# A hybrid decoder layer on one core: the first feed-forward takes seven products from group 2 and one down projection behind its groups, with its side work spread over the groups and the tables on GpSimd

## The chip, the cores and the metric

One core of a Trainium2 chip runs the whole layer in one launch. The metric is the device time in microseconds (us). The engines are TensorE (PE, with its weight loads apart as PEld), VectorE (DVE), ScalarE (ACT), GpSimd (POOL) and SyncE (SP), which issues nearly all transfers.

## The reference

Width 1024, 1024 tokens, feed-forward width 2816, one batch, float32 in and out.

```python
def swiglu(h, w_gate, w_up, w_down):
    return (jax.nn.silu(h @ w_gate) * (h @ w_up)) @ w_down
...
    c_act = jax.nn.silu(cond)
    mod = c_act @ w_mod[l] + b_mod[l]
    (sh1, sc1, g1, sh2, sc2, g2, sh3, sc3, g3) = jnp.split(mod, N_MOD, axis=-1)

    h = modulate(rms_norm(x, ffn1_norm[l]), sh1, sc1)
    x = x + 0.5 * g1[:, None, :] * swiglu(h, ffn1_w_gate[l], ffn1_w_up[l], ffn1_w_down[l])

    h = modulate(rms_norm(x, mix_norm[l]), sh2, sc2)
    proj = h @ w_in[l]
    b_gate, c_gate, v, u = jnp.split(proj, [D_CONV, 2 * D_CONV, 3 * D_CONV], axis=-1)
    y_conv = short_conv_mixer(b_gate, c_gate, v, conv_w[l])
    y_ssm = s5_mixer(u, lambda_re[l], lambda_im[l], log_dt[l], b_re, b_im, c_re, c_im, d_skip, glu_w, glu_b)
    y_mix = jnp.concatenate([rms_norm(y_conv, out_norm_conv[l]), rms_norm(y_ssm, out_norm_ssm[l])], axis=-1)
    x = x + g2[:, None, :] * (y_mix @ w_out[l])

    h = modulate(rms_norm(x, ffn2_norm[l]), sh3, sc3)
    x = x + 0.5 * g3[:, None, :] * swiglu(h, ffn2_w_gate[l], ffn2_w_up[l], ffn2_w_down[l])
    return rms_norm(x, final_norm)
```

`s5_mixer` is a diagonal state-space model over 32 groups of 16 channels with 64 states each; its discretized matrices follow from the inputs `lambda_re`, `lambda_im`, `log_dt`, `b` and `c`, so the kernel computes tables of them before the mixer. `mod` needs `w_mod`, 36 MB.

## The kernel before, in words

**Layout.** Activations lie with the model width on the partitions: `x[k][h]` is the k-th of 8 blocks of 128 rows by 512 tokens, `h` the half of the tokens; two blocks share a tile `xt[k // 2][h]`.

**A product.** Every value is split in a high part that the multiplier keeps exactly and a low rest. `mm3` makes a product of three matmuls, high by high, high by low, low by high, into one PSUM bank, and then ticks a clock. The split costs ScalarE a cast (`hi`) and VectorE a subtraction (`lo`). `Weights` does this as a stream: `load` brings raw weights on SP's queue into two buffers, `pump` splits them into the slots of a ring (`ringp`, three granules of 128x1024, for one stretch a fourth in `ring1`) as soon as `free` returns a slot.

**Groups.** A feed-forward runs over 11 groups of two column blocks of 128. A *direct* group makes gate and up with 192 matmuls of 128x512 (`gate_up`). A group in *seven products* (`seven`) multiplies 2x2 blocks by Strassen's scheme: seven products with sums of the activation's blocks (S1 to S4, made once by `combos`), and sums of weights, which `combine` makes on GpSimd with three operations per raw tile (one of 128x1024, two of 128x512); 168 matmuls per group, with the results added together on VectorE. After each group comes its part of the down projection: 96 matmuls (`down`, `down2`), added to `x`.

**The two feed-forwards differ.** `SEVEN_FROM = (6, 1)`: the first (FFN1) is direct in groups 0 to 5 and in seven products from 6; the second (FFN2) is direct in group 0 alone. FFN2 also has its down projection behind all groups (`down7`): the products' left blocks and their sums are stored to DRAM per group (`Left`), the sums of `w_down` are made on GpSimd per group (`right_sums`) and stored, and then seven passes (`PASSES`) of 11 blocks by four banks by three matmuls, 924, read both back.

**Side work.** `Clock` orders it: a generator in `clock.side` advances one step every `clock.period` products, and `clock.after(n, fn)` calls a function n products later. FFN1's `side1` has a period of 2 during groups 1 to 3: `ssm_base` makes the basic vectors of the state-space tables, then eight times `ssm_batch` (a batch of four state groups: `bb`, `cl`, `bl`, their products `kp` and transposes `tp` on TensorE, then the rotations `rot`) and three `mod_block`, each of two modulation vectors of 128x1024. All of this arithmetic is on VectorE. The gate G1 comes in the prologue (`gate1`).

```python
    clock.period = 2
    first_seven = SEVEN_FROM[0]
    for g in range(1, first_seven):
        ...
            clock.side.append(combos(act1, "h1", "BBBA", nc.gpsimd))
```

Each engine runs its instructions in the order written here, so the engine queues follow the code. Names in the profile: `fa` is FFN1 and `fb` FFN2 with the group's number behind, `g`, `u`, `d` gate, up and down, `A`, `B`, `C` the banks of the seven products, `D` the down projection behind the groups; `w` a split weight, `raw` a raw one, `sums` its sums, `wd` a piece of `w_down` in `right_sums`, `wm` a block of `w_mod`. Helpers hold most instructions of VectorE, ScalarE and TensorE on one line (L107), so the names tell them apart.

Of the kernel before, what the change touches and what calls it, by code (L numbers as in the profile page):

```python
# [34 lines left out]
SEVEN_FROM = (6, 1)  # L35
# [59 lines left out]


class InOrder:


    strict = False  # L100

    def __init__(self, tc, engine):
        self.tc, self.engine, self.last = tc, engine, None

    def __getattr__(self, name):
        def call(*args, **kw):
            r = getattr(self.engine, name)(*args, **kw)  # L107
            if self.last is not None and InOrder.strict:
                info = mybir.DependencyInfo(mybir.DependencyClass.NoSync, mybir.DependencyReason.DATA)
                self.tc.add_manual_dep(r.ins, self.last.ins.name, info, reason="order of issue")  # L110
            self.last = r
            return r

        return call
# [115 lines left out]
def hymba_layer(ctx: ExitStack, tc, x_d, wm1_d, wmod_d, gu1_d, gs1_d, wd1_d, win_d, wout_d, glu_d, gu2_d, gs2_d, wd2_d, cols_d, cond_d, lam_d, bc_d, out_d):  # L230
    nc = tc.nc
    V, A, T, SP = (InOrder(tc, e) for e in (nc.vector, nc.scalar, nc.tensor, nc.sync))
# [55 lines left out]
    def stream(gu, gs, wd, m):  # L288

        joined = m == 1  # L290
        plain([a for g in range(m) for a in (gu[2 * g], gu[2 * g + 1], wd[g])][: 3 * m - joined])
        for g in range(m, NGRP):
            j = len(srcs)
            inner = m - joined < g < NGRP - 1
            srcs.extend([gs[g - m, 0], wd[g - 1], gs[g - m, 1]] if inner else [gs[g - m, 0], gs[g - m, 1]])
            seven = [(i, c) for i in (j, j + 1 + inner) for c in Weights.SEVEN]
            seven = [seven[i : i + 2] for i in range(0, 14, 2)]
            if inner:
                granules.extend(seven[:1] + [[(j + 1, 2 * q), (j + 1, 2 * q + 1)] for q in range(2)] + seven[1:])
            else:  # L300
                granules.extend(seven)
        j = len(srcs)
        srcs.extend([wd[NGRP - 2], wd[NGRP - 1]])
        granules.extend([(i, 2 * q), (i, 2 * q + 1)] for q in range(2) for i in (j, j + 1))

    stream(gu1_d, gs1_d, wd1_d, SEVEN_FROM[0])
# [145 lines left out]
    def norm_into(act, h, ss, n, name, where="A"):  # L452


        def use(bc):
            got = []
            for k in range(KT):
                clock.after(k, lambda k=k: got.append(modulated(k, h, bc, n, name, where)))
            act[h] = got
# [1204 lines left out]
```

## Time and profile before

| what | value |
|---|---|
| median of three runs | 1779.12 us (1778.97 to 2155.73) |
| profiled execution, own time | 1781.04 us |
| its span | 1779.3 us |
| PE busy | 1703.8 us, 96% |
| DVE busy | 1214.9 us, 68% |
| ACT busy | 520.4 us, 29% |
| POOL busy | 302.9 us, 17% |
| DMA | 245.52 MB, mean 138 GB/s |

The stages by time from the start of the span: prologue and the start of group 0 to 73; FFN1 to 784 (groups 0 to 3 to 351, 4 and 5 to 484, seven products from there); the mixer to about 1106; FFN2 after that, its down projection from 1548. A row of a window gives busy time and the number of instructions per engine in that stretch; a row of the waits gives who waits (engine, tile), for whom, the sum in us, how often, and the longest or the mean; a row of the groups gives shapes, count, busy time, the mean in ns, and the idle time ahead. Idle time of an engine that is not the bound costs nothing.

### The profile page before, as it was taken

To read this page: it belongs to the slowest core of one execution; us is meant where nothing else is said; L and a number is where in the kernel's file an instruction comes from. 1 tells how busy PE (TensorE), PEld (TensorE's weight loads), DVE (VectorE), ACT (ScalarE), POOL (GpSimd) and SP (SyncE) were. 2 spreads that over 40 slices of the span, in tenths; PEclk is the share of its full clock that TensorE was granted. 3 is DMA by queue.
4 is the path that set the end of the run, shared out by engine and by line. 5 is a ranking of instruction groups with operands and counts; after the bars stand their busy time and mean duration, and the time that the engine had idled before them with its cause. 6 is when DMAs were issued, how large, how long until landed. Compare 5 with 4: busy or idle time off the path is not lost.

```text
span 1779.3 us, 20370 instructions
## 1 busy us (share of the span) xinstructions
PE 1703.8 (96%) x7724; PEld 1407.8 (79%) x7724; DVE 1214.9 (68%) x2109; ACT 520.4 (29%) x765; POOL 302.9 (17%) x187
## 2 busy tenths in 40 slices
PE   4998989999999999999999999979999999999997
PEld 3786767788788888877888888858888888888887
DVE  7999999937755666573665845986676566656564
ACT  4311212112232223333122623422233232344440
POOL 0000000001512122020000021133555443201020
PEclk9998999999999999999999999989999999999998
DMA  7625565410021111313564131134454444677632
GB/s 313 230 72 178 197 218 193 167 62 30 24 71 48 48 48 58 127 48 106 180 211 124 48 118 52 63 119 162 175 186 181 152 144 165 215 267 255 245 125 95
DMA packets 102771, 245.52 MB, mean 138 GB/s; under 512 B 16913, under 2 KB 32529, under 8 KB 89362
## 3 DMA queue, kind: packets, MB, share of 16 engines
q1 hardware_dynamic: 102674, 244.23, 39.4%
q8 instruction: 60, 0.98, 0.2%
q14 instruction: 37, 0.30, 0.1%
HBM read 185.21 MB, written 54.79 MB: 135 GB/s over the span
## 4 chain that ended last, share of the span: by engine, by line
PE 74%; DVE 3%; POOL 1%; DMA 1%; ACT 1%; issue 1%; SPq 0%; DVEq 0%; ACTq 0%; POOLq 0%
PE fbDX L107 7%; PE fbDY L107 5%; PE wo L107 5%; PE b L107 2%; PE v L107 2%; PE c L107 2%; PE fa10d L107 2%; PE u L107 1%; PE fb0u L107 1%; PE fa5u L107 1%; PE fb0g L107 1%; PE fa8d L107 1%; PE fa7d L107 1%; PE fa6d L107 1%; PE fa4d L107 1%; PE fa4u L107 1%
## 5 line engine op out<-in xcount | busy, mean ns | idle before, releaser
L107 DVE TENSOR_TENSOR w<-raw,w 128x1024 fp32r<-128x1024 f32 (+1 forms) x220 | 256.6, 1179 | 123.2 <-ACT w L107 122.1
L107 ACT CAST w<-raw 128x1024 fp32r<-128x1024 f32 (+1 forms) x220 | 188.7, 873 | 513.5 <-POOL raw L170 58.1
L169 POOL TENSOR_TENSOR sums<-raw 128x1024 f32<-128x1024 f32 x30 | 80.7, 2689 | 846.8 <-PE fa5u L107 436.7
L107 PE MATMUL fbDX<-fbLh,w 128*128 128x512 f32 (+1 forms) x440 | 115.4, 349 | 0.0
L107 DVE TENSOR_TENSOR w<-sums,w 128x512 fp32r<-128x512 f32 x90 | 64.0, 729 | 44.7 <-ACT w L107 44.4
L107 PEld LDWEIGHTS fbDX<-fbLh,w 128*128 128x128 f32 x440 | 78.0, 191 | 10.4
L107 PE MATMUL fbDY<-fbLh,w 128*128 128x512 f32 x264 | 81.8, 389 | 0.0
L107 ACT CAST w<-sums 128x512 fp32r<-128x512 f32 x90 | 52.8, 619 | 95.6 <-PE fa8d L107 9.7
L107 PE MATMUL fbDX<-fbLl,w 128*128 128x512 f32 (+1 forms) x220 | 76.7, 349 | 0.0
L107 DVE TENSOR_TENSOR fbLl<-fbLr,fbLh 128x1024 fp32r<-128x1024 f32 (+1 forms) x42 | 48.9, 1172 | 15.8 <-ACT fbLh L107 14.5
L107 PEld LDWEIGHTS fbDY<-fbLh,w 128*128 128x128 f32 x264 | 49.6, 188 | 10.3
L107 DVE CUSTOM_DVE_ANT_0 wm<-wm,cact 128x1024 f32<-128x1024 f32 x48 | 57.6, 1211 | 0.0
L388 POOL TENSOR_TENSOR n3aq<-n3aq,n3aq 128x512 f32<-128x512 f32 x5 | 6.5, 1292 | 266.7 <-ACT n3aq L107 266.5
L107 PE MATMUL fbDY<-fbLl,w 128*128 128x512 f32 x132 | 51.3, 389 | 0.0
L388 POOL TENSOR_TENSOR n_0q<-n_0q,n_0q 128x512 f32<-128x512 f32 (+1 forms) x10 | 13.8, 1377 | 200.6 <-ACT n_0q L107 200.3
L107 PEld LDWEIGHTS fbDX<-fbLl,w 128*128 128x128 f32 x220 | 42.1, 191 | 5.1
L107 PE MATMUL wo<-oa,w 128*128 128x512 f32 x192 | 45.4, 391 | 0.6 <-DVE w L107 0.6
L107 ACT CAST fbLh<-fbLr 128x1024 fp32r<-128x1024 f32 (+1 forms) x42 | 40.5, 976 | 18.6 <-DMA fbLr<-l_d 18.0
L107 PE MATMUL u<-h,w 128*128 128x512 f32 x192 | 44.8, 392 | 0.8 <-DVE w L107 0.8
L107 PE MATMUL v<-h,w 128*128 128x512 f32 x192 | 45.4, 393 | 0.0
L107 PE MATMUL c<-h,w 128*128 128x512 f32 x192 | 45.2, 392 | 0.0
L107 PE MATMUL wo<-ob,w 128*128 128x512 f32 x192 | 45.2, 391 | 0.0
(1021 smaller groups left out, 3930.7 us busy)
## 6 DMA issues: line engine op xcount, KB each, us to landing
raw<-in_gs SPq DMA_DIRECT2D x30, 1024.0 KB, 4.8
wm<-in_wmod SPq DMA_DIRECT2D x24, 1024.0 KB, 5.2
fbLr<-l_d SPq DMA_DIRECT2D x35, 512.0 KB, 6.6
raw<-in_wd SPq DMA_DIRECT2D x17, 1024.0 KB, 5.2
raw<-in_gu SPq DMA_DIRECT2D x14, 1024.0 KB, 4.9
wd<-in_wd SPq DMA_DIRECT2D x22, 512.0 KB, 4.3
t_d<-wd SPq DMA_DIRECT2D x22, 512.0 KB, 2.7
mw<-in_wm SPq DMA_DIRECT2D x8, 1024.0 KB, 8.3
```

The lines of the kernel that those rows point to most:

```text
L107: r = getattr(self.engine, name)(*args, **kw)
L169: self.G.tensor_tensor(out=f[:, :1024], in0=r[:, 512:1536], in1=r[:, :1024], op=ALU.subtract)
L388: nc.gpsimd.tensor_tensor(out=a, in0=a, in1=sq[:, :n], op=ALU.add)
```

## The change

**FFN1 as FFN2.** `SEVEN_FROM` becomes (2, 1). FFN1's groups 0 and 1 stay direct, 2 to 10 are in seven products; none has a down projection of its own. Left blocks go to `l1_d`, the sums of `w_down` to `t1_d`, and `down7` runs behind the groups.

**Left sums in place.** `modulated` may write its product over `x` (`over=True`), and `combos` makes S1 to S4 by scalar-and-tensor operations in those tiles. `x` is read again later: in FFN1 from the input, in FFN2 from `x2_d`, stored block by block in `w_out`.

**Side work.** `ssm_batch` runs on GpSimd, its rotations apart (`ssm_rot`, on GpSimd too) in `side2` during `down7` with a period of 6. The modulation vectors, G1 with them, are fetched in single blocks of 128x1024: four per batch during the groups (32), 24 during `down7`. `side1` starts behind group 1 with a period of 3. `right_sums` issues its four operations 8, 12, 16 and 20 products later and its stores after 24. The prologue no longer loads G1; the fourth ring slot opens only ahead of `down7`. The u projection of the first half takes its weights one after another. The class `InOrder` goes; its flag had no effect here.

```diff
-SEVEN_FROM = (6, 1)
+SEVEN_FROM = (2, 1)
...
+    t1_d, t2_d = (scratch.tile([4, KH, P, HALF], F32, name=f"t{n}_d")[:] for n in (1, 2))
+    l1_d, l2_d = (scratch.tile([7, KH, P, HALF], F32, name=f"l{n}_d")[:] for n in (1, 2))
...
+    stream7(gu1_d, gs1_d, wd1_d, t1_d, SEVEN_FROM[0])
...
-    def combos(act, name, homes, engine=None):
+    def combos(act, n, name):
...
+        def pair(out, a, s, b, op0, op1):
+            for i in range(2):
+                V.scalar_tensor_tensor(out=out[:, i, :], in0=a[:, i, :], scalar=s[:, i : i + 1], in1=b[:, i, :], op0=op0, op1=op1)
+
+        for j in range(2):
+            (t11, t21), (t12, t22) = xt[j], xt[j + 2]
+            pair(t22, t21, both[:, 2 * j :], t22, ALU.add, ALU.add)
             yield
+            V.tensor_tensor(out=t21[:], in0=t11[:], in1=t21[:], op=ALU.subtract)
             yield
+            pair(t11, t22, mods[:, n, 2 * j :], t11, ALU.subtract, ALU.subtract)
             yield
+            pair(t12, t12, mods[:, n, 4 + 2 * j :], t11, ALU.add, ALU.subtract)
             yield
+            split("S2", j, t11)
             yield
...
+        for i, op in enumerate(ops):
+            clock.after(8 + 4 * i, op)
...
+        clock.after(24, stores)
...
     def ssm_batch(b):
...
-            V.tensor_tensor(out=dst, in0=la[0], in1=sc[0], op=ALU.mult)
-            V.tensor_tensor(out=t, in0=la[1], in1=sc[1], op=ALU.mult)
+            G_.tensor_tensor(out=dst, in0=la[0], in1=sc[0], op=ALU.mult)
             yield
-            V.tensor_tensor(out=dst, in0=dst, in1=t, op=op)
+            G_.tensor_tensor(out=t, in0=la[1], in1=sc[1], op=ALU.mult)
+            yield
+            G_.tensor_tensor(out=dst, in0=dst, in1=t, op=ALU.add)
...
     def side1():
+        mod_fetch("B")
         with tc.tile_pool(name="sb1", bufs=1) as sb1:
             yield from ssm_base(sb1)
...
         for b in range(NB):
-            yield from ssm_batch(b)
+            for i, _ in enumerate(ssm_batch(b)):
+                yield
+                if i % 3 == 1:
+                    mod_next("B")
+                    yield
+
+    def side2(rp):
+        for b in range(NB):
+            for _ in ssm_rot(b, rp):
+                yield
             for _ in range(3):
-                yield from mod_block()
+                if fetched:
+                    mod_next("A")
+                    yield
...
+    clock.period = 3
     clock.side.append(side1())
...
+    lefts = Lefts(l1_d, "faL")
+    left = this
+    for g in range(SEVEN_FROM[0], NGRP):
+        this = Left(l1_d, g, f"fa{g}", "B")
+        hooks = {("g", 1): [left.sums], ("g", 5): [lambda g=g: right_sums(g - 2, wd1_d, t1_d, "B")]}
+        if g < 4:
+            hooks["u", 5] = [lambda g=g: right_sums(g + 7, wd1_d, t1_d, "B")]
...
+        seven(f"fa{g}", this, hooks)
+        left = this
...
+    clock.period = 6
+    clock.side.append(side2(es1.enter_context(tc.tile_pool(name="rp", bufs=1))))
...
+    down7(lefts, 0, "faD", after1, None, beside1)
```

What GpSimd has in its queue during FFN1's groups in seven products before: nothing but the weights' sums, three rows per raw tile.

```order
L169 TENSOR_TENSOR sums20_4102<-raw20_3966 128x1024
L170 TENSOR_TENSOR raw20_3966<-sums20_4102,raw20_3966 128x512
L171 TENSOR_TENSOR sums20_4102<-raw20_3966 128x512
L169 TENSOR_TENSOR sums22_4351<-raw22_4181 128x1024
L170 TENSOR_TENSOR raw22_4181<-sums22_4351,raw22_4181 128x512
L171 TENSOR_TENSOR sums22_4351<-raw22_4181 128x512
```

And GpSimd after, in about group 5, around table batch 2:

```order
L1043 TENSOR_TENSOR bl2_2301<-tab2_1136,bb2_2292 128x512
L1045 TENSOR_TENSOR blt2_2334<-tab3_1137,bb2_2292 128x512
L1043 TENSOR_TENSOR cl2_2411<-tab0_1134,prm2_2279 128x576
L1047 TENSOR_TENSOR bl2_2301<-bl2_2301,blt2_2334 128x512
L149 TENSOR_TENSOR sums11_2384<-raw11_2189 128x1024
L1045 TENSOR_TENSOR clt2_2412<-tab1_1135,prm2_2279 128x576
L150 TENSOR_TENSOR raw11_2189<-sums11_2384,raw11_2189 128x512
L1047 TENSOR_TENSOR cl2_2411<-cl2_2411,clt2_2412 128x576
L151 TENSOR_TENSOR sums11_2384<-raw11_2189 128x512
L606 TENSOR_TENSOR wd3_1_2482<-wd3_1_2482,wd3_0_2481 128x512
L607 TENSOR_TENSOR wd3_0_2481<-wd3_0_2481 128x512
```

The table operations (`bl`, `cl` and their second terms) now stand between the three sums of a raw weight, and the right sums (`wd`) behind them.

VectorE before, in the direct group 2, with table operations, modulation vectors (ISA, `wm`) and a weight's split (`w`):

```order
L107 TENSOR_TENSOR bb_1935<-bb_1938,bb_1939 128x64
L107 TENSOR_TENSOR clt_1947<-tab_888,prm_1933 128x576
L107 TENSOR_TENSOR bl_1962<-tab_889,bb_1935 128x512
L107 TENSOR_TENSOR cl_1946<-cl_1946,clt_1947 128x576
L107 TENSOR_TENSOR w_2158<-raw_1857,w_2158 128x1024
L107 TENSOR_TENSOR blt_1963<-tab_890,bb_1935 128x512
L107 TENSOR_TENSOR bl_1962<-bl_1962,blt_1963 128x512
L107 TENSOR_TENSOR dg_1997<-ident,lam 16x64
L107 ISA wm_3_2090,ms_3_2111<-wm_3_2090,cact 128x1024
```

VectorE after, in group 4, now in seven products, with the left sums of group 3 (`fa3s`):

```order
L519 TENSOR_TENSOR fa4gu_2043<-fa4gt_2026,fa4gB 128x512
L182 TENSOR_TENSOR w_2049<-raw_1715,w_2049 128x512
L182 TENSOR_TENSOR w_2049<-raw_1851,w_2049 128x512
L438 ISA wm_5_2001,ms_1688<-wm_5_2001,cact 128x1024
L438 ISA ms_1688 128x1
L590 TENSOR_TENSOR fa3s_2058<-fa3l_1951 128x512
L591 TENSOR_TENSOR fa3s_2058<-fa3l_1882,fa3l_1951 128x512
L519 TENSOR_TENSOR fa4gu_2101<-fa4gt_2026,fa4gB 128x512
L182 TENSOR_TENSOR w_2103<-raw_1851,w_2103 128x512 x2
L519 TENSOR_TENSOR fa4gu_2101<-fa4gu_2101,fa4gC 128x512
```

No table product is left on VectorE there; one modulation vector stands between two weights, and the left sums are new.

TensorE after, in group 5, where a table batch is used (`h1S` is a piece of the left sums):

```order
L321 MATMUL fa5uB<-h1S_1_642,w_2439 128x512
L322 MATMUL fa5uB<-h1S_1_642,w_2439 128x512
L323 MATMUL fa5uB<-h1S_1_642,w_2439 128x512
L1063 MATMUL kp_2532<-cl_2411,bl_2301 16x128 x4
L1068 MATMUL tp_2537<-ident,bl_2301 128x128 x4
L321 MATMUL fa5uB<-h1S_2_718,w_2439 128x512
```

The products `kp` read `cl` and `bl` from GpSimd's queue above and stand in the middle of a bank's accumulation; before, they stood in groups 1 to 3 and read them from VectorE.

More of the change, by code (lines that the diff above doesn't have):

```diff
@@ L890, in hymba_layer @@
                 part(h, k, (0, 1, 2))
[L892 to L897 removed]
+    left = Left(l1_d, 0, "fa0", "B")
     for i in range(3):
@@ new lines, in hymba_layer @@
+    groups_open = ExitStack()
+    clock.period = 3
+    clock.side.append(combos(act1, 0, "h1"))
+    this = Left(l1_d, 1, "fa1", "B")
+    for fi in range(2):
+        (wg,) = ws.take()
+        pg = [proj(wg, act1[h], f"fa1g{fi}_{h}") for h in range(2)]
+        ws.free()
+        if fi == 0:
+            left.sums()
+        (wu,) = ws.take()
+        for h in (1, 0):
+            gu_evac(fi, h, pg[h], proj(wu, act1[h], f"fa1u{fi}_{h}"), this, f"fa1_{fi}_{h}")
+        ws.free()
+    sums_open = groups_open.enter_context(sums_opened())
@@ L1249, in hymba_layer @@
+    down7(lefts, 0, "faD", after1, None, beside1)
+    while clock.side:
+        clock.step()
     es1.close()
```

430 lines of the change are left out of this document (155 added, 275 removed).

## The prediction

> **What bounds the kernel now.** I read the engine totals first, then the slices, then the stages.
>
> ```profile
> PE 1703.8 (96%) x7724; PEld 1407.8 (79%) x7724; DVE 1214.9 (68%) x2109; ACT 520.4 (29%) x765; POOL 302.9 (17%) x187
> ...
> PE   4998989999999999999999999979999999999997
> ...
> DVE  7999999937755666573665845986676566656564
> ...
> POOL 0000000001512122020000021133555443201020
> PEclk9998999999999999999999999989999999999998
> ```
>
> TensorE is busy for 96% of the span, so only two things can pay: fewer matmuls, or the few slices that are not full. VectorE stands at 9 in slices 1 to 7, just where TensorE shows its eights, and GpSimd is empty there. Next come the stages. Behind each window: its length, then busy time and instruction count of PE, PEld, DVE, ACT and POOL, the granted clock, and the DMA share and rate.
>
> ```profile
> core 0: us, PE busy (x) PEld busy (x) DVE busy (x) ACT busy (x) POOL busy (x), PEclk, DMA share, GB/s
> 73.46:350.68 277.22, 254.08 (x1105) 203.20 (x1104) 269.61 (x719) 49.67 (x70) 0.00 (x0) 0.95 0.52 177
> ...
> 459.48:483.50 24.02, 22.52 (x98) 17.93 (x97) 21.31 (x24) 5.10 (x8) 11.04 (x7) 1.00 0.00 0
> 483.50:739.20 255.70, 255.70 (x1130) 211.80 (x1129) 151.01 (x208) 75.05 (x120) 47.06 (x27) 1.00 0.17 59
> ...
> 1105.80:1205.40 99.60, 89.17 (x377) 72.37 (x377) 84.81 (x128) 35.52 (x57) 22.64 (x13) 0.95 0.27 96
> 1205.40:1548.00 342.60, 342.60 (x1513) 283.77 (x1512) 219.74 (x279) 105.10 (x173) 155.96 (x91) 1.00 0.48 170
> 1548.00:1726.00 178.00, 178.00 (x787) 147.44 (x786) 107.84 (x105) 78.26 (x88) 14.79 (x9) 1.00 0.67 237
> ```
>
> The first is the end of group 0 and groups 1 to 3 of the first feed-forward (FFN1): the only long stage where VectorE (269.6 of 277.2 us) and not TensorE is full. The second is the down projection of group 5 and the third groups 6 to 10, seven products each, without a gap. The fourth is the start of the second feed-forward (FFN2), with VectorE full again; the fifth its groups in seven products, the sixth its down projection.
>
> ```profile
> 527.04 21.76 PE fa6d L107 x96
> ```
>
> This row of the chain of waits gives the price of a 128x512 matmul where nothing waits: 21.76/96 = 0.2267 us. The third window confirms it: five groups of 168 and three down projections of 96 make 1128 matmuls, times 0.2267 = 255.7 us. All sums below stand against the profiled execution's own 1781.04 us (span 1779.3), which is 1.9 above the median of the runs shown.
>
> **Term 1: fewer matmuls, -51.7 us.** A direct group takes 192 for gate and up, a group in seven products 168; groups 2 to 5 change over: 4 x 24 = 96 fewer. FFN1's down projection was 96 per group, 1056; as seven passes of 11 x 4 x 3 it is 924, so 132 fewer. That is 228 x 0.2267 = 51.7 us. Nothing hides a matmul on a full engine, so this term is the firmest.
>
> **Term 2: the idle time early in FFN1, -39.8 us.** The first window holds 1008 matmuls of 128x512 (48 left of group 0, its down projection, three groups of 288): 228.5 us, so 48.7 us are something else. The waits name it.
>
> ```profile
> PE kp L107 <- DVE bl L107: 11.5, 5, 4.8
> PE fa2d L107 <- DVE x L107: 5.2, 3, 2.6
> ...
> 232.49 1.03 PE L107 MATMUL kp<-cl,bl 128*16 128x128 f32 x8 [1.56 <-DVE bl L107]
> 233.45 0.66 PE L107 MATMUL tp<-ident,bl 128*128 128x128 f32 x4
> 233.87 7.08 PE L107 MATMUL fa2u<-h,w 128*128 128x512 f32 x30
> ```
>
> The table products' own matmuls (kp, tp) take 1.4 us, from 232.49 to 233.87, for each of eight batches: 11.1 us that remain, later. The other 37.6 us are TensorE behind VectorE. What leaves VectorE there comes from the groups by shape:
>
> ```profile
> L107 DVE CUSTOM_DVE_ANT_0 wm<-wm,cact 128x1024 f32<-128x1024 f32 x48 | 57.6, 1211 | 0.0
> L107 DVE TENSOR_TENSOR cl<-tab,prm 128x576 f32<-128x576 f32 x8 | 6.0, 748 | 0.0
> L107 DVE TENSOR_TENSOR cl<-cl,clt 128x576 f32<-128x576 f32 x8 | 6.0, 747 | 0.0
> L107 DVE TENSOR_TENSOR rot<-rs,rb 128x512 f32<-128x512 f32 x16 | 17.4, 1090 | 0.5 <-PE tp L107 0.5
> L107 DVE TENSOR_TENSOR rot<-rot,rott 128x512 f32<-128x512 f32 x16 | 10.8, 677 | 0.0
> L107 DVE TENSOR_TENSOR f<-f,f 128x512 f32<-128x512 f32 x24 | 16.4, 683 | 0.1
> ```
>
> The modulation vectors are 57.6; the tables three operations of 0.75 and, by the last row's duration, three of 0.68 per batch, 34 in all; the rotations 17.4 + 10.8 and as much again as the first for their second product, 45. Some 137 of 269.6 us go from these groups, half of VectorE's load, and the idle time with them: -37.6. In the second window TensorE waits for the last right sums of the old preparation: 24.0 us against 96 x 0.2267 = 21.8, so -2.2 more. Bounds: if VectorE still lags, none of it comes back.
>
> **Term 3: the start of FFN2, -10 us.** The fourth window holds 360 matmuls (81.6 us) and an estimated 1.6 of 17 small ones; 16.4 us are lost with VectorE at 84.8 of 99.6. The old combinations are 36 additions of 128x512, 36 x 0.68 = 24.6 us. The new ones are 12 of 128x512 and two of 128x1024; at 0.68 and twice 0.68 that is 10.9, so 13.7 us go. Not all of it stands on the path: I take -10, with ends 0 and -16.4. The stores of x issued earlier on SP's queue move eight transfers ahead of the norm, which starts at least eight ticks (24 matmuls, 5.4 us) later; I cost them at nothing, and if that cover failed they would delay the first in-place write by one landing.
>
> **Term 4: what the new order makes late, +34 us.** Three places and a clock.
>
> Group 2 now meets the table base on VectorE while act1's left sums are just done. Adding the queue of VectorE from the last piece of act1 to group 2's end, at this trace's durations, gives 105 us; TensorE needs 103 for its some 455 matmuls there. With GpSimd's interference on top I take +8 (0 to +20).
>
> Groups 3 to 10 put the tables and the right sums on GpSimd, beside two combinations of weights per group. The trace shows what the two engines do to each other:
>
> ```profile
> 540.04 2.40 POOL L169 TENSOR_TENSOR sums<-raw 128x1024 f32<-128x1024 f32 x1 [27.28 <-DVE w L107]
> 542.52 1.29 POOL L170 TENSOR_TENSOR raw<-sums,raw 128x512 f32<-128x512 f32 x1
> 543.89 1.30 POOL L171 TENSOR_TENSOR sums<-raw 128x512 f32<-128x512 f32 x1
> ...
> 1314.29 0.69 DVE L107 TENSOR_TENSOR fb4uu<-fb4uu,fb4uC 128x512 f32<-128x512 f32 x1 [1.76 <-PE fb4uC L107]
> 1315.00 1.58 DVE L107 TENSOR_TENSOR w<-raw,w 128x512 fp32r<-128x512 f32 x1
> 1316.50 1.77 DVE L107 TENSOR_TENSOR fb4l<-fb4uu,fb4gu 128x512 f32<-128x512 f32 x1
> ...
> 1314.73 1.29 POOL L677 TENSOR_TENSOR wd<-wd 128x512 f32<-128x512 f32 x1
> 1316.11 1.61 POOL L678 TENSOR_TENSOR wd<-wd,wd 128x512 f32<-128x512 f32 x1
> 1317.80 1.63 POOL L679 TENSOR_TENSOR wd<-wd,wd 128x512 f32<-128x512 f32 x1
> ```
>
> GpSimd alone takes 1.37 us from start to start (542.52 to 543.89); beside VectorE's additions of two SBUF operands it takes 1.69 (1316.11 to 1317.80), and VectorE's 0.68 becomes 1.58 to 1.77. An addition with a PSUM operand keeps its 0.69. So each VectorE operation of that kind costs GpSimd about 0.33 us, and VectorE about 1.
>
> Per group GpSimd has two combinations (2.40 + 1.29 + 1.30 and gaps, 5.2 each) 10.4, right sums of four operations 5.5, and a table batch: three large ones of 512 at 1.37, three of 576 at an estimated 1.52 (1.29 x 576/512 and the gap), six of 128x64, which the trace does not show on GpSimd, at 0.3 (between 0.16, an eighth of 1.29, and 1.29 itself; nearer the former, by size): 10.5, and as a batch takes 48 of a group's 56 ticks, 1.15 of them, 12.0. That is 27.9 us. VectorE has some 25 two-operand operations per group, the four long ones of the modulation counted twice: 29 x 0.33 = 9.6. Together 37.5 of the 39.7 us that TensorE needs (168 x 0.2267 and 1.15 x 1.4). The fifth window has GpSimd at 46% and no wait; here it is at 94%, and TensorE's queue holds kp behind the last table operation, with the group's matmuls behind kp. Slack of 2 us in a queue where combinations for the next weights stand between table operations is too little for every batch; I take 2.5 us per group, +20. The ends are 0 and, if no two such operations overlap at all, 27.9 + 21 x 0.68 + 4 x 1.21 = 47.0 against 39.7: 7.3 x 8 = +59. The weights' ring holds about two granules (11 us) ahead, which covers single stalls, and by the overlap seen above the sum is nearer the lower end.
>
> The down projection gets 24 modulation vectors (29 us) and the rotations on GpSimd (48 operations, some 66 us). Scaled from the sixth window, VectorE had 127 us in 209.5; with 29 more it is at 74%. +2 (0 to +15).
>
> Each stall lowers the granted clock for a while (0.95 in the first and fourth windows): +4 (0 to +8).
>
> **Sum.** -51.7 - 39.8 - 10 + 34 = -67.5: 1713.5 of own time, 1711.6 against the median. Costed at nothing: the 44 left stores and 22 more transfers of right sums in FFN1 (DMA is busy 52% in the first window and 17% in the third; FFN2 carries the same at 48%), the removed prologue loads (behind x and the first weights anyway), and the u projection in another order.
>
> **The rivals.**
>
> *GpSimd and VectorE serialize fully* (chance 0.16). Then GpSimd's queue is the bound of groups 3 to 10, +59 instead of +20: 1781.04 - 67.5 + 39 - 1.9, about 1750. For it: each VectorE row beside GpSimd loses a whole 1 us. Against: the pair above takes 1.69 us and not 1.37 + 0.68 = 2.05, so 0.36 us of it overlap. The Trainium skill, page "SBUF — State Buffer", section "Who interferes with whom", calls the ports that the two engines share an exclusive lock: whoever comes first has them for the whole instruction, and the other fully blocks. By that rule the pair would take the whole 2.05 us and the kernel this rival's time; the trace agrees that they block each other, and not that they do so for the whole instruction.
>
> *Everything hides* (0.18). The waits of term 4 don't arise, as in the third and fifth windows: -51.7 - 39.8 - 10, about 1678, to 1690 with some. For it: two stages of that shape ran at 0.2267 per matmul. Against: neither had tables on GpSimd.
>
> *VectorE still lags early* (0.06): the base, act1's sums and the splits of two weights per granule keep TensorE waiting, term 2's 37.6 don't come back: 1749.
>
> *Slower: GpSimd's table operations are slow.* Their operands are strided and broadcast in four dimensions, which no GpSimd row of this trace is. On VectorE that cost nothing for cl (748 against 747 ns) but 1090 against 677 for rot. 48 large table operations stand on the path through kp; at 2.8 us each instead of 1.4 they eat the whole 67.5, and from 3.5 us the kernel is over 2% slower, 1815 and more. A factor of 1.6, as for rot, gives 2.2 us and 1750; 2.5 would be needed. Chance 0.04.
>
> **How the numbers follow.** The forecast has 0.56, with a range of its own of 1690 to 1740 from the bounds of its terms. Over all cases I take 1678 (everything hides) to 1750 (full serialization), which leaves out the upper half of two rivals, the slow side and what lies under 1678. A measurement tells about 2% from no change: below 1743.5 is faster, above 1814.7 slower. Faster: forecast 0.55, everything hides 0.18, and the lower part of the 1750 cases 0.07, so 0.80; slower 0.04; the rest 0.16.
>
> **What would show it.** FFN1, from 73.46 to 784.42 before (711 us), should take about 654. Waits of kp for a GpSimd table row of 1 to 3 us in groups 3 to 10 are term 4; FFN2's start should shrink from 99.6 to about 90. Large table rows on GpSimd should read 1.3 to 1.8 us, VectorE's w<-raw of 128x512 about 1.2 in these groups. I am wrong if kp waits over 5 us per batch, if TensorE shows no wait at all in groups 3 to 10, or if group 2 takes over 60 us.

## The result: 0.8% slower, not 3.8% faster

The changed kernel takes 1792.36 us (median of 4 runs, 1791.31 to 1795.81) against 1779.05 of the kernel before: a ratio of 1.0082, 95% interval [1.0063, 1.0102]. The forecast was 1712 with a range of 1678 to 1750. One of the four executions of the kernel before ran in a slower state, 2155.73 us, and the ratio leaves it out. The profiled execution of the changed kernel spans 1790.1 us, 10.8 more than before.

The engine totals and slices of the page of the changed kernel:

```profile
PE 1662.8 (93%) x7496; PEld 1369.0 (76%) x7496; DVE 1266.2 (71%) x1911; ACT 567.2 (32%) x824; POOL 601.1 (34%) x387
...
PE   4996988877989898999999999999999999999997
...
DVE  7999888777767788774465663986676556656564
...
POOL 0103877746751974100000002133455443201020
PEclk9998999988999999999999999999999999999998
```

TensorE is busy 41 us less, so the matmuls are gone as counted (7496 instructions for 7724). But the span is longer: in slices 3 to 15, counted from 0, many of TensorE's digits are 8 or less and so are three of its clock's, and there GpSimd now has most of its work. The stages of the changed kernel, by windows (columns as in the prediction): group 0's end and group 1; group 2; groups 3 to 10; the down projection; the start of the second feed-forward.

```profile
74.55:128.95 54.40, 54.40 (x241) 45.05 (x240) 53.20 (x220) 15.54 (x28) 6.01 (x3) 1.00 0.28 93
128.95:184.86 55.91, 41.29 (x169) 32.97 (x168) 53.95 (x152) 13.37 (x23) 20.25 (x13) 0.88 0.43 145
184.86:570.39 385.53, 337.31 (x1442) 269.74 (x1440) 298.56 (x340) 103.97 (x172) 247.57 (x179) 0.94 0.60 202
570.39:808.00 237.61, 218.46 (x942) 178.68 (x941) 186.39 (x193) 86.74 (x98) 109.13 (x57) 0.96 0.71 253
1128.58:1216.41 87.83, 85.01 (x378) 69.12 (x377) 75.05 (x109) 36.27 (x58) 23.23 (x13) 1.00 0.26 96
```

Groups 0 and 1 run without a gap, 54.40 us for 240 matmuls. Groups 3 to 10 take 385.5 us where their matmuls, tables' products included, need 8 x 39.7 = 317.6. The down projection takes 237.6 for 209.5. All of FFN1 takes 808.00 - 74.55 = 733.5 us, before 711.0: +22.5; FFN2's start -11.8; the rest is unchanged within 1.2. That is the 10.8 us.

The waits of TensorE in groups 3 to 10, the four longest, and of VectorE over the whole span:

```profile
PE fa8gB L321 <- DVE fa8gu L519: 9.4, 1, 9.4
PE fa7gB L321 <- DVE fa7gu L519: 9.1, 1, 9.1
PE fa9uB L321 <- DVE fa9uu L519: 5.2, 1, 5.2
PE fa6gB L321 <- DVE fa6gu L519: 4.9, 1, 4.9
...
DVE wm L438 <- DMA wm<-in_wmod: 31.5, 13, 5.9
```

The view has 16 rows, 48.3 us in sum, which is TensorE's whole idle time there (385.53 - 337.31 = 48.2). All are waits for a read by VectorE, and none is of kp for GpSimd or of a matmul for its weights. Nearly all stand at the second use of bank B, once or twice per group: the fourth product may not add to the bank until VectorE has read the second. VectorE's timeline at the border of groups 7 and 8 shows why that read is late (the last row is the read):

```profile
426.26 0.68 DVE L519 TENSOR_TENSOR fa7ut<-fa7ut,fa7uB 128x512 f32<-128x512 f32 x1
426.98 0.69 DVE L513 TENSOR_TENSOR fa7l<-fa7ut,fa7gt 128x512 f32<-128x512 f32 x1
431.01 1.23 DVE L438 CUSTOM_DVE_ANT_0 wm<-wm,cact 128x1024 f32<-128x1024 f32 x1 [3.34 <-DMA wm<-in_wmod]
...
434.57 0.69 DVE L590 TENSOR_TENSOR fa7s<-fa7l 128x512 f32<-128x512 f32 x1
435.17 2.83 DVE L591 TENSOR_TENSOR fa7s<-fa7l,fa7l 128x512 f32<-128x512 f32 x1
437.92 1.75 DVE L592 TENSOR_TENSOR fa7s<-fa7s,fa7l 128x512 f32<-128x512 f32 x1
439.59 1.22 DVE L429 TENSOR_TENSOR mods<-ms,cols 128x8 f32<-128x8 f32 x1
440.73 0.68 DVE L593 TENSOR_TENSOR fa7s<-fa7l,fa7s 128x512 f32<-128x512 f32 x1
441.33 0.67 DVE L519 TENSOR_TENSOR fa8gu<-fa8gt,fa8gB 128x512 f32<-128x512 f32 x1
```

TensorE had left that bank at about 430. Ahead of its read stood a modulation vector that waited for its block, the last read of bank C and the product behind it, two splits of weights, and four left sums, of which one took 2.83 us and one 1.75 instead of 0.69; even an addition of 128x8 took 1.22. GpSimd was in its weights' sums at that moment:

```profile
434.73 2.72 POOL L149 TENSOR_TENSOR sums<-raw 128x1024 f32<-128x1024 f32 x1 [4.70 <-DVE w L182]
437.53 1.59 POOL L150 TENSOR_TENSOR raw<-sums,raw 128x512 f32<-128x512 f32 x1
439.20 1.59 POOL L151 TENSOR_TENSOR sums<-raw 128x512 f32<-128x512 f32 x1
```

and TensorE's row behind it carries the wait:

```profile
442.06 0.80 PE L321 MATMUL fa8gB<-h1S,w 128*128 128x512 f32 x1 [9.36 <-DVE fa8gu L519]
```

Group 2 and the down projection have waits of their own:

```profile
PE fa2gB L321 <- DVE fa2gu L519: 13.6, 1, 13.6
PE faDY L322 <- DVE faLl L643: 9.6, 4, 7.1
PE faDX L322 <- DVE faLl L643: 6.8, 1, 6.8
```

In group 2 left sums and some 30 small operations of the tables' base stand ahead of VectorE's read; beside GpSimd one of 128x64 took 2.36 us instead of 0.22. In the down projection TensorE waits for the split of a left block, and ScalarE, which begins that split, waited 59.3 us there for the blocks' loads, against 18.0 in the down projection of the second feed-forward before.

### The profile page after: what moved, and what is told of

Read it like the earlier page. It is cut to its first block, busy times and chain, and to the rows that moved or that the text cites. A ratio compares the mean times of both kernels' runs of the same rounds, so it can differ in the third digit from the quotient of the medians.

```text
span 1790.1 us, 20465 instructions
## 1 busy us (share of the span) xinstructions
PE 1662.8 (93%) x7496; PEld 1369.0 (76%) x7496; DVE 1266.2 (71%) x1911; ACT 567.2 (32%) x824; POOL 601.1 (34%) x387
## 4 chain that ended last, share of the span: by engine, by line
PE 51%; DVE 3%; issue 0%; DMA 0%; ACT 0%; POOL 0%; DVEq 0%; ACTq 0%
PE fbDX L323 2%; PE fbDX L322 2%; PE fbDX L321 2%; PE fbDY L323 2%; PE fbDY L322 2%; PE fbDY L321 2%; PE wo L323 1%; PE wo L321 1%; PE wo L322 1%; PE b L321 1%; PE v L322 1%; PE b L322 1%; PE c L322 1%; PE v L323 1%; PE v L321 1%; PE c L323 1%
## 5 line engine op out<-in xcount | busy, mean ns | idle before, releaser
L182 DVE TENSOR_TENSOR w<-raw,w 128x1024 fp32r<-128x1024 f32 (+1 forms) x249 | 310.6, 1260 | 120.3 <-ACT w L181 119.5
L350 POOL TENSOR_TENSOR n3aq<-n3aq,n3aq 128x512 f32<-128x512 f32 x5 | 6.5, 1291 | 269.3 <-ACT n3aq L346 269.1
L350 POOL TENSOR_TENSOR n_0q<-n_0q,n_0q 128x512 f32<-128x512 f32 (+1 forms) x10 | 13.8, 1378 | 200.5 <-ACT n_0q L346 200.3
L321 PE MATMUL fbDX<-fbLh,w 128*128 128x512 f32 (+1 forms) x220 | 77.1, 351 | 0.0
L323 PE MATMUL fbDX<-fbLh,w 128*128 128x512 f32 (+1 forms) x220 | 77.1, 350 | 0.0
L322 PE MATMUL faDX<-faLl,w 128*128 128x512 f32 x176 | 70.2, 399 | 6.8 <-DVE faLl L643 6.8
L643 DVE TENSOR_TENSOR faLl<-faLr,faLh 128x1024 fp32r<-128x1024 f32 (+1 forms) x42 | 63.0, 1504 | 13.9 <-ACT faLh L642 13.9
L321 PE MATMUL faDX<-faLh,w 128*128 128x512 f32 x176 | 70.1, 399 | 0.0
L323 PE MATMUL faDX<-faLh,w 128*128 128x512 f32 x176 | 69.9, 397 | 0.0
L322 PE MATMUL faDY<-faLl,w 128*128 128x512 f32 x132 | 52.6, 398 | 9.6 <-DVE faLl L643 9.6
L642 ACT CAST faLh<-faLr 128x1024 fp32r<-128x1024 f32 (+1 forms) x42 | 40.7, 976 | 60.0 <-DMA faLr<-l_d 59.3
L151 POOL TENSOR_TENSOR sums<-raw 128x512 f32<-128x512 f32 x38 | 58.2, 1531 | 2.7
L150 POOL TENSOR_TENSOR raw<-sums,raw 128x512 f32<-128x512 f32 x38 | 55.6, 1463 | 2.5
L321 PE MATMUL faDY<-faLh,w 128*128 128x512 f32 x132 | 51.9, 394 | 0.0
L323 PE MATMUL faDY<-faLh,w 128*128 128x512 f32 x132 | 51.9, 393 | 0.0
```

Source lines behind the costliest of these rows:

```text
L150: self.G.tensor_tensor(out=r[:, 512:1024], in0=f[:, 512:1024], in1=r[:, :512], op=ALU.add)
L151: self.G.tensor_tensor(out=f[:, 1024:], in0=r[:, 1536:], in1=r[:, 512:1024], op=ALU.subtract)
L182: self.V.tensor_tensor(out=lo, in0=src, in1=hi.bitcast(F32), op=ALU.subtract)
L321: T.matmul(out, lhsT=hi, rhs=ah, start=first, stop=False, skip_group_check=more)
L322: T.matmul(out, lhsT=hi, rhs=al, start=False, stop=False, skip_group_check=more)
L323: T.matmul(out, lhsT=lo, rhs=ah, start=False, stop=last, skip_group_check=more)
```

## The experiments

Four theories. G, of the prediction: GpSimd's queue is the bound. Q: SyncE's queue stands behind stores of GpSimd's results, so loads are late. B: a burst of VectorE at a group's border stands ahead of the read that TensorE waits for. V: VectorE's time as a whole, its own work and what GpSimd's reads add. The expectations also name S (the side work alone makes FFN1 late), P (the seven products with their left and right sums do so by themselves) and T (the tables on GpSimd do it through its queue, the weights' sums and SyncE's stores). "Groups" are groups 3 to 10 with the busy time of VectorE and GpSimd in them, "down" the down projection of FFN1; all from windows of each profile. Experiments without an interval are single runs beside a run of the kernel before at 1779 to 1780.

| run | groups, us | VectorE | GpSimd | down | time |
|---|---|---|---|---|---|
| changed kernel | 385.5 | 298.6 | 247.6 | 237.6 | 1792.4 |
| e1 stores on GpSimd's queue | 397.6 | 307.8 | 257.4 | 239.9 | 1808.8 |
| e2 no modulation loads | 389.1 | 300.0 | 245.2 | 238.0 | 1798.9 |
| e3 left sums later | 396.9 | 297.0 | 243.7 | 235.2 | 1803.5 |
| e4 no tables | 354.5 | 269.3 | 149.2 | 235.0 | 1759.9 |
| e5 no side work | 319.8 | 214.1 | 138.8 | 211.3 | 1705.9 |
| e6 no modulation | 339.5 | 238.0 | 227.5 | 226.7 | 1739.0 |
| e7 no right sums | 370.3 | 272.2 | 181.0 | 244.0 | 1780.0 |
| e8 tables on VectorE | 378.1 | 320.3 | 154.3 | 236.4 | 1785.8 |
| e9 tables write only | 353.5 | 270.4 | 220.2 | 238.3 | 1760.2 |
| e12 half modulation | 361.0 | 275.8 | 237.5 | 235.6 | 1766.9 |

### e1 to e3: queue, loads, order

```diff
 e1: -SP.dma_start(mo_d[b]..., cl4...)     +nc.gpsimd.dma_start(...)   (also t_d and co_d, si_d in FFN1)
 e2: -SP.dma_start(r[:], wmod_d[...])
     -tensor_tensor_reduce(out=w, in0=w, in1=cact[:], ...)   +tensor_tensor_reduce(out=w, in0=cact[:], in1=cact[:], ...)
 e3: -hooks = {("g", 1): [left.sums], ...   +hooks = {("g", 3): [left.sums], ...
```

> Stores of results of GpSimd (cl, right sums of the first feed-forward, rotations) go out on GpSimd's own queue instead of SyncE's; nothing else changes. Theory Q (SyncE's queue stands behind these stores, so modulation blocks and raw weights land late and VectorE waits for them): the waits of VectorE for wm, 13 us in the groups and 22 us behind them, go, and the kernel falls by 30 to 60 us to 1730-1760. Theory B (VectorE's burst at a group's end stands ahead of the eviction that TensorE waits for): 0 to -10 us in the groups, so 1775 or more. Theory G (GpSimd itself is the bound): no change, or slower by the issue of 54 transfers.

> The 56 modulation blocks are not loaded; the same VectorE operation reads the condition vector twice instead, so the vectors are not the reference's. Theory Q: VectorE's waits for wm (35 us in all) go and SyncE's queue is shorter: -25 to -45 us. Theory B: VectorE's burst stays as long, only the waits inside it go: -10 to -25 us. Theory G: 0.

> The left sums of the group before are issued behind the fourth product of gate instead of the second (order alone). Theory B: the eviction of gB no longer stands behind the four left sums (6.5 us with GpSimd beside); the waits for it at the start of groups 3 to 9, 37 us in all, fall by half or more: -15 to -35 us. Theories Q and G: within 5 us of 1792.

None of the three is faster; they are 6 to 16 us slower, by one run each. e1 doesn't settle Q, since VectorE still waited 15.7 us for wm. e2 does: without the loads VectorE's wait for them cannot be, and the groups stay at 389.1; in the down projection (238.0 against 237.6) another wait took its place:

```profile
DVE faLl L642 <- ACT faLh L641: 35.7, 11, 9.3
```

(13.9 us in the changed kernel, for the split of the left blocks). For the groups theory Q falls: of the raw weights' loads one alone is late there in the changed kernel, ScalarE waiting 4.0 us for it. For the down projection it stays open, since the left blocks come late there. e3 moves the left sums behind the fourth of the gate's products, and TensorE waits longer for the same reads (11.4 and 11.0 us in groups 7 and 8); so it is not these four rows alone that are in the way, and the narrow form of theory B falls too.

### e4 to e8: what costs

```diff
 e4: the G_.tensor_tensor rows of ssm_batch and comb are left out; kp, tp and mo_d read ident
 e5: e4, and no wm loads, no mod_vector, no rotations
 e6: no wm loads, no mod_vector
 e7: -("g", 5): [right_sums ...], hooks["u", 5] = [right_sums ...]; T1 to T4 are read from wd1_d
 e8: -G_ = nc.gpsimd   +G_ = V      (in ssm_batch)
```

> The twelve table operations per batch on GpSimd are left out (TensorE's kp and tp and the store of cl read a constant tile), so the state-space tables are not the reference's. Theory G: the whole excess of groups 3 to 10 goes, -50 to -68 us. Theory Q: the 44.6 us that SyncE's queue waits for cl go: -20 to -35 us. Theory B: VectorE's operations get shorter by what GpSimd's neighbours cost them, -15 to -30 us, and the waits for the evictions at a group's start remain in part.

> Tables, rotations and all 56 modulation vectors (loads and arithmetic) are left out; the seven products, the left and right sums and the down projection stay, so only the mixer's inputs are not the reference's. If the side work is all that makes the first feed-forward late (theory S), groups 3 to 10 take 39.7 us each or less (38.1 with kp and tp beside) and the down projection 211: 1792 - 68 - 26 - some of group 2 = about 1690. If the seven products with left and right sums in this place are late by themselves (theory P), the groups stay above 43 us and the kernel above 1735.

> Only the modulation vectors are left out, loads and arithmetic (59 us of VectorE in the groups, 36 behind them). Without the loads alone nothing was gained. Theory B (VectorE's in-order work, of which these are the longest pieces, stands ahead of evictions): groups 3 to 10 fall from 385 to 340-350 us and the down projection from 238 to 220: 1725 to 1745. Theory T (the tables on GpSimd make the stretch late through the sums of weights): groups stay at 370 or more, 1770.

> The right sums of the first feed-forward are left out (22 loads, 44 GpSimd operations and 22 stores; the down projection reads plain blocks of w_down in their place, so its result is not the reference's). GpSimd stood 37.7 us at their loads in groups 3 to 10, with the sums of weights behind. Theory T: without them the sums come in time, -25 to -45 us. Theory B: VectorE has fewer neighbours on GpSimd, -10 to -20 us.

> The twelve table operations per batch go back to VectorE in the same place. It gets 8 x (6 x 0.7 + 6 x 0.15) = 41 us more of its own and loses GpSimd's neighbours and SyncE's waits for cl. Theory B: as VectorE decides, a little slower or the same as 1792, 1785 to 1805. Theory T: faster, 1760 to 1775, near the run without tables.

Without tables, rotations and modulation vectors (e5) a group of 3 to 10 takes 40.0 us on average, TensorE being busy for 39.7 of it, and the down projection 211.3. For these stages theory S and the prediction's price for the bare work hold. For group 2 they don't: e5 keeps the tables' base, and its wait is there in full (13.6 us, and 13.5 to 13.8 in e1 to e4, e6 and e8; 9.6 in e7). No run takes the base out, so the cause in group 2 is read from the timeline alone. Its windows of groups 3 to 10 and of the down projection:

```profile
186.75:506.59 319.84, 317.93 (x1429) 260.41 (x1428) 214.05 (x271) 104.42 (x172) 138.78 (x82) 0.99 0.53 184
506.59:717.89 211.30, 211.30 (x941) 175.30 (x940) 126.52 (x140) 87.05 (x98) 14.09 (x9) 1.00 0.63 218
```

Of the 65.7 us that the side work adds to the groups, the modulation vectors are worth 46.0 (e6) and the tables 31.0 (e4); together that is more than all, so the two overlap. Against theory G: GpSimd keeps 227.5 us of work in e6, and 46.0 of the 65.7 us are gone. Right sums (e7) are worth 15 in the groups and 4 in group 2, and the down projection gave 6 back. And e8 is the plainest lesson: it takes 93 us off GpSimd and puts only 22 on VectorE's balance, and the kernel gets a little faster (1785.8, one run). Against e4 without tables, VectorE is busy for 29.3 us more with them on GpSimd and for 51.0 us more with them on itself: the move had saved it less than half.

### e9, e12: occupancy, or VectorE's time

```diff
 e9:  -G_.tensor_tensor(out=dst, in0=la[0], in1=sc[0], op=ALU.mult)   +twice G_.memset(dst, 0.0)    (all six)
 e12: -mod_vector(r[:], ...)   +mod_vector(r[:, :512], ...)           (reduced against cact[:, :512])
```

> The six large table operations per batch on GpSimd become two constant writes each, into the same tiles: GpSimd reads nothing there, and the tables are not the reference's. What the tables cost without them was 32 us. Theory V (VectorE is the bound of these groups by its own work and by what GpSimd's reads of two-operand neighbours add; with the tables it is busy 327 us of the 318 that TensorE needs): its busy time falls to 290-300 us and the kernel to 1755-1770, as without tables. Theory T (occupancy of GpSimd's queue and SyncE's waits for cl): time stays at 1780 or more.

> Each modulation vector is computed from the first 512 of its 1024 columns, so the vectors are not the reference's; loads, order and number of instructions stay. Theory V: VectorE loses about 25 us in groups 3 to 10 and 15 behind; at 0.7 us of time per us (what leaving all of it out gave) that is -17 and -7, 1765 to 1772. If the instructions' places and loads count and not their length: within 5 us of 1792.

In e9 GpSimd writes the same large tiles and reads nothing for them. It stays busy for 220.2 us of the groups, 71 more than in e4 without tables, and the groups take the same (353.5 and 354.5), with the same time of VectorE (270.4 and 269.3). Theory T falls with it: 71 us more of GpSimd's time cost nothing. It is GpSimd's reading that costs, and as TensorE's waits are all for VectorE, it costs through VectorE. The window of e9:

```profile
184.13:537.63 353.50, 326.54 (x1441) 261.84 (x1440) 270.37 (x340) 104.12 (x172) 220.15 (x227) 0.99 0.66 221
```

The Trainium skill, page "SBUF — State Buffer", section "Who interferes with whom", says that a VectorE instruction with two SBUF inputs contends with a GpSimd instruction that reads SBUF and not with one that only writes it. The trace agrees: 270.4 us of VectorE with the writes, 269.3 without the tables at all. (The expectation's 327 us were a sum of durations, which overlap by some 0.1 us each; the window's 298.6 is the busy time.)

e12 keeps each load, instruction and place, and halves the length of the modulation vectors. VectorE's time falls by 22.8 us and the groups by 24.5. Theory V holds with a slope of about 1, though VectorE is busy for only 77% of that stretch. The timeline at groups 7 and 8 suggests how: what stands on the path is the work between the last product of a group and the first reads of the next, and in the other part VectorE waits for TensorE.

### e10, e13 to e16: the side work elsewhere

```diff
 e10: -if i % 3 == 1:   +if i % 3 == 1 and i // 3 < 1:      (8 vectors in the groups, 16 in the down projection)
      +def side3(): ...mod_next("A")                         (32 in the mixer)
 e13: 24 in the down projection, 24 in the mixer, a step every 12 products
 e14: e13 and e8;   e15: e10 with a step every 4 products in the groups and 10 in the mixer, and 3 empty steps before kp instead of 4;   e16: e15 and e8
```

> Of the 56 modulation vectors 8 stay in the groups, 16 in the down projection behind them, and 32 move into the mixer's u, c and v stages, where VectorE has room; the result stays the reference's. Theory V: by the runs without modulation (46 us less in the groups for 32 vectors, 11 less behind them for 24) 24 fewer give -30 to -40 and 8 fewer -2 to -6; the mixer gives back 0 to 10: 1745 to 1765, faster than the kernel before. If only the loads or the order counted, 1785 or more.

> As e10 (8 modulation vectors in the groups), but 24 in the down projection behind them and only 24 in the mixer, one every 12 products up to the middle of the output projection; the result stays the reference's. Theory V: groups as in e10 (359), down projection as in the changed kernel (238), mixer +3 to +10 instead of +20: 1765 to 1775, faster than the kernel before by 0.3 to 0.8%.

> As e13, with the table operations back on VectorE as in e8. With 24 modulation vectors fewer VectorE has room in the groups. Theory V: it gains 28 us of VectorE time in the groups (e8 against the changed kernel) at 0.7: +10 to +20 against e13, unless that room takes it: 1765 to 1790. If GpSimd's table operations cost more by what they block on the way (weights' sums, SyncE's stores) than by VectorE's time: faster than e13.

> The changed kernel with its side work spread evenly: one table batch and one modulation vector per group of seven products (a step every 4 products instead of 3, so the batches fill all groups), 16 vectors in the down projection behind them, 32 in the mixer, one every 10 products. The result stays the reference's. Theory V: VectorE's time in groups 3 to 10 stays about 268 us, but no group has over 40 of it: 340 to 350 us instead of 359 (e10); down projection 230; mixer +10 to +14: 1755 to 1768, faster than the kernel before by 0.6 to 1.4%. If the crowding of single groups doesn't matter: 1775 to 1780.

> As e15, with the table operations on VectorE. By e14 against e13 (-7 us) it is a little faster than e15: 1750 to 1763. If it was GpSimd that e14 relieved by an earlier sum of weights, the gain is the same; if VectorE's added time counts in full (28 us more by e8): 10 to 20 us slower than e15.

| run | groups | VectorE | down | time | ratio to before |
|---|---|---|---|---|---|
| e10 | 359.1 | 246.4 | 229.9 | 1778.3 | 0.9995 [0.9985, 1.0005] |
| e13 | 357.4 | 248.3 | 243.4 | 1785.2 | 1.0030 [1.0019, 1.0041] |
| e14 | 354.2 | 285.8 | 243.5 | 1777.9 | 0.9988 [0.9976, 1.0001] |
| e15 | 351.5 | 241.3 | 238.5 | 1784.7 | 1.0026 [1.0012, 1.0040] |
| e16 | 349.3 | 285.9 | 239.6 | 1779.5 | 1.0007 [0.9995, 1.0019] |

The groups gain 26 to 36 us, e10 and e15 a little less than said. The mixer, from u to the second feed-forward, takes back 20 us in e10, 11 in e13 and e14, 23 in e15 and 20 in e16; e13 and e14 lose 6 more in the down projection. Its window from u to w_out in the changed kernel and in e10:

```profile
808.00:1023.96 215.96, 213.07 (x1058) 179.65 (x1057) 121.60 (x218) 56.78 (x84) 2.93 (x2) 1.00 0.49 152
```

```profile
773.73:1009.43 235.70, 219.99 (x1057) 182.54 (x1056) 158.13 (x287) 57.66 (x85) 4.17 (x2) 0.98 0.67 206
```

VectorE was at 56% there, and 36 us more of it came with 20 us more of time. The 32 vectors bring their loads along (DMA share 0.67 for 0.49), and of TensorE's waits in e10 5.8 us are for VectorE (yy) and 7.6 are px's, 3.4 of them for a transfer and the rest for nothing that the profile shows; so vectors and loads are not separated. The expectations for e10, e13, e15 and e16, 1745 to 1775, were wrong in this: a stage with room on average is no free place, and a wider spacing (e15) didn't help. The slope of theory V also fails across these runs (e10 has 24 us less of VectorE than e9 and is 6 us slower in the groups), as it does in e8, e14 and e16: it holds where VectorE's work is taken away in place, not where the order around it changes. Why the groups still take some 30 us more than in e5 stays open. None of the five is clearly faster than the kernel before (the intervals of e10, e14 and e16 hold 1); e13 and e15 are 0.3% slower.

### e11: only the tables on GpSimd, in the kernel before

```diff
-V.tensor_tensor(out=dst, in0=la[0], in1=sc[0], op=ALU.mult)   +nc.gpsimd.tensor_tensor(...)   (comb and rot, 96 operations)
```

> The kernel before with one change: the tables' large products and the rotations, 96 operations, on GpSimd instead of VectorE, in its direct groups 1 to 3, where 37.6 us of TensorE were lost behind VectorE. Theory V with the price seen in the seven-product groups (GpSimd's operations cost VectorE more than half of what they take off it): VectorE's 269.6 us fall by about 35, and the kernel by 15 to 30 us, 1750 to 1765. If GpSimd's work were free for VectorE, it would fall by 79 us and the kernel by the whole 37: 1742. If the queue of SyncE and the waits for kp decide: no gain.

1817.6 us, a ratio of 1.0207 [1.0190, 1.0223]: a miss. VectorE's time fell in that stage as expected, from 269.6 to 231.0 us, but the stage grew from 277.2 to 301.5: the old generator issues kp right behind the tables:

```profile
PE kp L107 <- POOL bl L1119: 49.4, 8, 7.4
```

Here is the wait that the prediction looked for in the changed kernel. There, four empty steps stand between the last table operation and kp, and kp never waits; no run takes them out. With the same steps it waits once in e10 (6.6 us) and once in e13 (4.5 us).

### e17, e18: the second feed-forward alone

```diff
 e17, in the kernel before: +def combos_in_place(act, n, name): ...; modulated(..., over=True) for h3;
      +SP.dma_start(x2_d[h, :, d - 1 : d + 1, :], xt[d // 2][h][:])   (in w_out)
      +both = const.tile([P, 4], F32, ...)
 e18: e17 with   -both = const.tile([P, 4], F32, ...)   +both = g1s      (an old tile of 8 columns)
```

> The kernel before with one part of the change alone: in the second feed-forward the left sums are made in place of x and x is stored block by block in the output projection. Theory: the start of that feed-forward falls from 99.6 to 88 us as in the changed kernel and nothing else moves: 1779 - 12 = 1765 to 1770, faster by 0.5 to 0.8%. If that gain in the changed kernel came from what stands elsewhere (steps of another period, freed buffers): 1775 or more.

> As e17, with the sum of the shifts kept in a tile that already exists, so the weights' ring stands at the addresses of the kernel before (a multiple of 64 bytes; in e17 32 bytes beside it). If the place of the ring made every matmul 2.8% longer: groups of 168 take 38.1 us again, the start of the second feed-forward about 87, and the kernel 1765 to 1769, faster than before by 0.6 to 0.8%. If something else in that part of the change slows TensorE: 1795 to 1800 as e17.

e17 took 1799.85 us, 1.0116 [1.0101, 1.0131], although FFN2's first two groups fell from 99.6 to 87.2. The chain shows the reason; the same 96 matmuls of group 6's down projection, in e17 and in e18:

```profile
531.01 22.40 PE fa6d L107 x96
```

```profile
524.19 21.76 PE fa6d L107 x96
```

0.2333 us per matmul against 0.2267. The only difference is a tile of 16 bytes per partition in a constant pool, which by the program's allocation moves the weights' ring from byte 202752 of each partition to 202720, 32 bytes off a multiple of 64 (the raw weights and scratch tiles with it, which hardly a matmul reads). e17's own trace holds the comparison too. In the down projection of its second feed-forward some weights lie in tiles that did not move: 240 matmuls of 128x512 that read these start 0.2269 us apart, the 552 that read the moved ones 0.2333. Their activations lie at multiples of 64 in both. e18 takes **1764.77 us, a ratio of 0.9915 [0.9902, 0.9929]**: the fastest version that computes the whole layer, from one part of the change alone.

## Why the prediction was wrong, step by step

- **Term 1 (-51.7)** held: e5 shows the bare groups at 39.7 us of TensorE's time and the down projection at 211.3, against 209.5 counted.
- **Term 2 (-39.8)** held where it was: groups 0 and 1 have no gap. The side work's price came back in the groups behind.
- **Term 3 (-10)** held: -11.8 in the changed kernel. In e18 that stage takes 86.2 us instead of 99.6, 13.4 of the 15.4 that the whole kernel gains; the rest of its profiled execution's gain lies in FFN1, which the edit doesn't touch.
- **Term 4 (+34)** failed: it measured 17.8 in group 2 (8 forecast), 67.9 in groups 3 to 10 (20, upper end 59) and 28.1 in the down projection (2, upper end 15): 113.8. The 80 us between are the whole miss. The lower clock, a term of 4 (upper end 8), is in these figures: TensorE's busy time exceeds the counted matmuls by 3.2, 19.7 and 9.0 us, some 32, and its idle time is the other 82.

The step that failed in term 4 is its choice of engine for groups 3 to 10: it took GpSimd's queue for the bound and put the waits at kp behind it, where none came. It read the right rows, 0.33 us on GpSimd and "about 1" on VectorE for each pair, and summed the first alone. GpSimd came out at 37.5 us per group and measured 30.9 (247.57/8); it never was the bound. VectorE's sum was not made: with the prediction's own 29 operations at 1 us on top of FFN2's 24.4 us per group (219.74 us in 342.60, times 38.1) it is 53 us against 39.7. That sum would have named the engine, not the size: VectorE measured 37.3, under the 39.7, as not every operation has a neighbour. What was priced nowhere is its order: VectorE's work stands in bursts ahead of the reads that free bank B, and 48.2 us of waits came of it, with 19.7 of lower clock on top. The modulation vectors show what a neighbour costs:

```profile
L438 DVE CUSTOM_DVE_ANT_0 wm<-wm,cact 128x1024 f32<-128x1024 f32 x32 | 59.1, 1847 | 13.4 <-DMA wm<-in_wmod 9.9 <-DMA l_d<-fa6l 3.3
```

1847 ns in the groups against 1211 before. For group 2 the mechanism was right, VectorE's queue behind the tables' base, and only the size off, within its bounds. For the down projection 74% of VectorE was costed without neighbours, with 93 us of rotations reading beside it on GpSimd, and the left blocks' loads were costed at nothing; e5 shows that the side work makes the 26 us between 237.6 and 211.3, e6 that the modulation vectors make 11 of them, and which of neighbours and loads it is stays open.

None of the three signs of being wrong came up: kp never waited, TensorE had its waits, and group 2 took 55.9 us. They were signs for the engine that was expected; only FFN1's total, 733.5 us where 654 were forecast, spoke.

The rivals: "everything hides" was refuted, "full serialization", 1750, names the wrong queue. The slower rival came out on the right side and nearest in time by a wrong mechanism: GpSimd's tables took 1.2 to 1.75 us, not 2.8, and kp did not wait for them in the changed kernel. "VectorE still lags" was priced for the first groups only; it was the right engine, later.

## What to carry to other kernels

When work moves from VectorE to GpSimd, make the sum for VectorE as well: GpSimd's operations that read SBUF lengthened VectorE's two-operand ones here, by more than half of what the move took off it (29.3 of 51.0 us). An engine at 77% can be the bound when its work stands in bursts ahead of the reads that free a bank; look at what is queued ahead of each such read, and halve an operation in place to see whether its length counts. And try each part of a change alone: here one part was worth 0.85%, and hid behind another that lost more. Compare the place of the big tiles as well, since a new tile of 16 bytes cost 2%.

## What the runs showed of the hardware

- The place of a tile counts: with the weights' ring 32 bytes off a multiple of 64, each 128x512 matmul that reads it took 0.2333 us instead of 0.2267 (e17, e18; 0.2333 and 0.2269 within e17), 2.9%.
- Waits are paid twice. TensorE's granted clock was 0.94 in groups 3 to 10 with 48.2 us of waits, and its busy time 337.3 us against 317.9 without them at 0.99 (e5): 19 us more. The Trainium skill, page "TensorE: Matmul & The Clock Gate", section "HAM oscillation — how this bites in real kernels", says that pauses over some 3.4 us send the clock back to half rate. The trace agrees on the half rate: with the wait of 9.36 us in group 8 the granted clock is 0.50 from 436.2 to 446.3. It differs on the length, and the measurement decides: the clock is 0.50 behind some shorter waits too, from 265.5 to 268.8 behind one of 1.98 us, and in the kernel before from 262.8 to 269.6 behind one of 2.64. The prediction had 4 us for it in all.
- GpSimd's writes alone cost VectorE nothing that a window shows (e9: 270.4 us busy against 269.3 in e4).
